# Forgetting attention in a two-layer decoder trunk: query products and the minus of weight pieces at other places in a hand-written order

## Chip, cores and metric

One core of a Trainium2 chip. The metric is the device time of one execution in microseconds (us), as the median of several runs.

## What is computed

The program is a whole two-layer decoder trunk on a residual stream of 512 tokens and 1024 features: a layer with dilated window attention and a gated convolutional feed-forward part, then a layer with forgetting attention and a second feed-forward part. The change lies in the forgetting attention. Cut to that part (16 heads of 64, blocks of 128 queries):

```python
def fox_mixer(xn, w_q, w_o, k, v, c):
    q = (xn @ w_q).reshape(B, T, B_HEADS, HEAD_DIM)
    ...
    for i in range(T // BLK):
        q0, q1 = i * BLK, (i + 1) * BLK
        s = jnp.einsum('bqhd,bkhd->bhqk', q[:, q0:q1], k[:, :q1]).astype(jnp.float32) * scale
        s = s + (c_t[:, :, q0:q1, None] - c_t[:, :, None, :q1])
        s = jnp.where(causal, s, NEG)
        p = jax.nn.softmax(s, axis=-1).astype(v.dtype)
        outs.append(jnp.einsum('bhqk,bkhd->bqhd', p, v[:, :q1]))
    o = jnp.concatenate(outs, axis=1)
    return o.reshape(B, T, B_WIDTH) @ w_o
```

Keys, values and the cumulative log-forget gates `c` are computed once, ahead of it.

## The kernel before

**Numbers.** Every float32 factor of a large product is split into a high part and a low part (the rest), and a product is three matmuls: high with high, high with low, low with high (`mm3`, lines 264 to 266). So each operand costs a copy on ACT (the high part) and a subtraction on DVE (the low part).

**Weights.** The class `Weights` hands out the weights in pieces of 128 x 1024. `load` issues the DMA of a raw piece on SP's queue; `high` copies it on ACT (line 57); `low` subtracts on DVE (line 69). In place of `low` there is a second way: `minus` writes the raw piece times -1 into the place of the low part on ACT (line 64), rounded as the high part is, and `low_added` issues a DMA on POOL's queue that adds the raw piece onto it (line 84), which leaves raw minus high. The four calls stand by hand in the attention loop.

**The loop.** A unit is (j, i): pair of heads j (0 to 7) and query block i (0 to 3), 32 units, in this order, and one pass of the loop issues for each unit, engine by engine in the order of the code (the schedule is manual, so each engine works in exactly this order):

- at i = 0, on SP: the load of the next pair's gates (`load_ck`);
- at i = 2, on PE: a part of the query product, then the 24 score matmuls (line 1578): 12 for blocks 2 and 3 of pair j, and 12 for blocks 0 and 1 of pair j + 1, and then the value products of the units finished so far (`values_of`, line 1627, 40 matmuls);
- on DVE: the reciprocal and the norm of the unit before (`f_norm`, lines 1598 and 1600);
- `f_exp`: on DVE the bias is added and the minimum taken (line 1588), on ACT the exponential with its sum (line 1590), for the two heads;
- on POOL: the bias of the next unit (`f_bias`, lines 1560 and 1561);
- the weight calls and the drains of the query product: `q_high` (ACT, line 1500) and `q_low` (DVE, line 1506);
- at i = 0, 1 and 3, on PE: one part of a query product;
- `f_transpose` of the unit two back: transposes on PE (line 1612) and the copies of the transposed probabilities on ACT (line 1614);
- copies of finished outputs, `f_out_high` on ACT (line 1637) and `f_out_low` on DVE (line 1641).

A query product for one pair is 24 matmuls in four parts of six (`q_part`, lines 264 to 266 with the tile `q_ps`):

```python
        for kc in (2 * i, 2 * i + 1):
            bh, bl = xs(xTq, kc, ALL)
            mm3(o, wh[:, kc, :], wl[:, kc, :], bh, bl, kc == 0, kc == KD - 1)
```

The parts serve as filling between the pieces of the attention, ahead of their pair: in the kernel before, three parts of pair 1 run ahead of the loop, and from there on the last part of pair j + 1 runs in (j,0), and three parts of pair j + 2 in (j,1), (j,2) and (j,3). After the last part `q_high` stands at the end of (j,0) and `q_low` in (j,1). From (6,1) on no part is left; from (6,3) on parts of the output projection (`po.both`, tile `acc`) fill the units.

**What is shared.** All tiles in PSUM, the query products, scores, transposes and outputs, take one of eight banks; the attention's tiles in SBUF (gates, bias, probabilities, raw pieces) take one of ten slots. A tile's first writer waits until the last reader of the slot's or bank's earlier tile is done.

Of the kernel before, what the change touches and what calls it, by code (L numbers as in the profile page):

```python
# [103 lines left out]
def trunk_kernel(ctx, tc, x, norm_gains, w_qkv_a, w_o_a, w_q_b, w_o_b, kv_norm, w_kvf, b_f,  # L104
# [11 lines left out]
    def t8(shape, dt=F32, name="t8"):  # L116
        return p8.tile(shape, dt, tag="t8", name=name)
# [4 lines left out]
    def t2(shape, dt=F32, name="t2"):  # L122
        return p2.tile(shape, dt, tag="t2", name=name)

    def bank(shape, name="bank"):
        return psp.tile(shape, F32, tag="ps", name=name)
# [76 lines left out]
    W = Weights(nc, new_raw, lambda: t8([128, 2, 1024], F32R, name="w"), pieces)  # L203
# [59 lines left out]
    def mm3(o, ah, al, bh, bl, first, last, shared=False):  # L263
        pe.matmul(o, ah, bh, start=first, stop=False, skip_group_check=shared)  # L264
        pe.matmul(o, ah, bl, start=False, stop=False, skip_group_check=shared)  # L265
        pe.matmul(o, al, bh, start=False, stop=last, skip_group_check=shared)  # L266
# [91 lines left out]
    def xs(xT, kc, s):  # L358
        return xT[0][kc // 4][:, kc % 4, s], xT[1][kc // 4][:, kc % 4, s]
# [1116 lines left out]
    def load_ck(j):  # L1476
        t = t4([128, 2, T], name="ck")
        s = cd[2 * j:2 * j + 2, :]
        sp.dma_start(t, bass.AP(tensor=s.tensor, offset=s.offset, ap=[[0, 128], [T, 2], [1, T]]))
        cks[j] = t  # L1480
# [4 lines left out]
    def q_part(j, i):  # L1485

        if j >= 8:
            return
        if i == 0:
            qps[j] = (bank([128, T], name="q_ps"), [t.rearrange("p (k c) -> p k c", k=8) for t in W.get()])  # L1490
        o, (wh, wl) = qps[j]
# [4 lines that stand above are left out]
    def q_high(j):  # L1496
        if j >= 8:
            return
        qT[j] = t8([128, 2, T], F32R, name="qst")
        act.copy(qT[j][:, 0], qps[j][0])  # L1500

    def q_low(j):
        if j >= 8:
            return
        o, t = qps.pop(j)[0], qT[j]
        dve.tensor_tensor(t[:, 1], o, t[:, 0].bitcast(F32), ALU.subtract)
# [48 lines left out]
    def f_bias(j, i):  # L1555
        n = (i + 1) * 128
        bias = t4([128, 2, T], name="bias")
        for hh in range(2):
            hd = 2 * j + hh
            pool.tensor_scalar(bias[:, hh, :n], cks[j][:, hh, :n], -1.0, cq[:, i, hd:hd + 1], ALU.mult, ALU.add)  # L1560
        pool.affine_select(bias[:, :, n - 128:n], bias[:, :, n - 128:n], pattern=[[0, 2], [-1, 128]],
                           compare_op=ALU.is_ge, fill=NEG, base=0, channel_multiplier=1)
        bia[j, i] = bias
# [3 lines left out]
    def f_scores(j, blocks):  # L1567
        wide = blocks[0] >= 2
        if not wide:
            both = [bank([128, 2, 256], name="s_ps") for _ in range(2)]  # L1570
        k = kst[j // 2][:, j % 2]
        for i in blocks:
            nn = max(256, (i + 1) * 128)
            sc[j, i] = [bank([128, T], name="s_ps") for _ in range(2)] if wide else [o[:, i] for o in both]
            for qp, kp in ((0, 0), (0, 1), (1, 0)):
                for hh in range(2):
                    own = slice(64 * hh, 64 * hh + 64)
                    pe.matmul(sc[j, i][hh][:, :nn], qT[j][own, qp, i * 128:(i + 1) * 128], k[own, kp, :nn],
                              start=qp + kp == 0, stop=qp == 1)

    def f_exp(j, i):
        n = (i + 1) * 128
        s = sc.pop((j, i))
        bias = bia.pop((j, i))
        p = t4([128, 2, T], name="prob")
        nm, ls = small(2, "nm"), small(2, "ls")
        for hh in range(2):
            dve.tensor_tensor_reduce(p[:, hh, :n], s[hh][:, :n], bias[:, hh, :n], -0.125, BIG, ALU.add, ALU.min,
                                     nm[:, hh:hh + 1])
            act.activation(p[:, hh, :n], p[:, hh, :n], AF.Exp, bias=nm[:, hh:hh + 1], scale=-1.0,  # L1590
                           accum_out=ls[:, hh:hh + 1])
        prob[j, i] = (p, ls)

    def f_norm(j, i):
        n = (i + 1) * 128
        p, ls = prob[j, i]
        rl = small(2, "rl")
        dve.reciprocal(rl, ls)
        for hh in range(2):
            dve.tensor_scalar(p[:, hh, :n], p[:, hh, :n], rl[:, hh:hh + 1], None, ALU.mult)  # L1600
# [3 lines left out]
    def f_transpose(j, i):  # L1604
        p, _ = prob.pop((j, i))
        for hh in range(2):
            if i >= 2 or hh == 0:
                o = bank([128, 4, 128], name="pT_ps")
                t = t2([128, 4, 128], name="pT")
            k0 = (i + 1) * hh if i < 2 else 0  # L1610
            for k in range(i + 1):
                pe.transpose(o[:, k0 + k, :], p[:, hh, k * 128:(k + 1) * 128], ident)  # L1612
            if i >= 2 or hh == 1:
                act.copy(t[:, :k0 + i + 1], o[:, :k0 + i + 1])
            pT[j, i, hh] = t[:, k0:k0 + i + 1]
# [16 lines left out]
    def f_out_high(j):  # L1632
        o = ops[j]
        if j % 2 == 0:
            OTb[j // 2] = t8([128, 2, 2, T], F32R, name=f"OTb{j // 2}")
        t = OTb[j // 2]
        act.copy(t[:, 0, j % 2, :], o)

    def f_out_low(j):
        o, t = ops.pop(j), OTb[j // 2]  # L1640
        dve.tensor_tensor(t[:, 1, j % 2, :], o, t[:, 0, j % 2, :].bitcast(F32), ALU.subtract)
# [3 lines left out]
    wo = W.n_get + 7  # L1645
    fill = [(kc, b) for b in range(2) for kc in range(4)]
    W.ahead, W.ahead_dma = 1, 1
    for i in range(3):
        q_part(1, i)
        if i == 0:  # L1650
            W.split(W.n_get + 1)
# [6 lines left out]
    def values_of(n):  # L1658
        nonlocal pv_next
        while pv_next < n - 2:  # L1660
            j, i = units[pv_next]
            pv_next += 1
            f_pv(j, i)
            if i == 3:
                outs.append(j)

    f_scores(0, (0, 1))
    for n in range(N + 3):
        live = n < N
        if live:  # L1670
            j, i = units[n]
            if i == 0 and j + 1 < 8:
                load_ck(j + 1)
            if i == 2:
                q_part(j + 2, 1)
                f_scores(j, (2, 3))
                if j + 1 < 8:
                    f_scores(j + 1, (0, 1))
                values_of(n)
        if 1 <= n <= N:  # L1680
            f_norm(*units[n - 1])
        if live:
            f_exp(j, i)
            if n + 1 < N:
                f_bias(*units[n + 1])
            if i == 1:
                q_low(j + 1)
                if 2 <= j < 6:
                    W.minus()
                    W.low_added()  # L1690
            if i == 2 and j < 2 or (j, i) >= (6, 2):
                W.low()
            if i == 3 and j:
                f_out_low(j - 1)
            if i != 2:
                q_part(j + 1 + (i > 0), (i + 3) % 4)
            if (j, i) in ((7, 1), (7, 2)):
                next(down1)
        if 2 <= n < N + 2:
            f_transpose(*units[n - 2])  # L1700
        if n >= N + 3 - len(fill):
            po.both(*fill[n - N - 3 + len(fill)])

        if n >= N and n % 4 in (0, 2):
            values_of(n)
        while outs:
            f_out_high(outs.pop())
        if live and i == 0:
            q_high(j + 1)
        if live and (i == (j < 2) if j < 6 else (j, i) >= (6, 1) and W.n_split < wo + 4):  # L1710
            W.high()

    for _ in range(2):
# [51 lines left out]
```

## Time and profile before

| | |
|---|---|
| median of 3 runs | 1112.32 us (1112.14 to 1112.51) |
| the profiled execution: its time | 1111.92 us |
| the profiled execution: its span | 1110.1 us, 18038 instructions |
| mean granted clock of TensorE | 0.998 |
| PE, DVE, ACT, POOL busy | 1100.2, 876.4, 660.5, 213.8 us |
| query products of the attention (tile `q_ps`) | first matmul at 597.3 us, last at 698.2 us of the span |

The profile is of one execution; its times are counted from the first instruction of the span. A row of a timeline gives the start, the duration, the engine, the line, the operation, the output and inputs by their names, the shape and how many instructions were merged; in brackets stands how long the engine was idle before and what ended that. PE is TensorE's matmuls, whose ends are modelled; ACT is ScalarE, DVE is VectorE, POOL is GpSimd, SP the engine that issues most DMAs. A row of the windows view gives a stretch, then for PE, weight loads, DVE, ACT and POOL the busy time and the number of instructions, then the granted clock, the busy share of the DMA engines and GB/s.

### The profile page before, as it was taken

What the parts mean: (1) busy time and instruction counts of PE and PEld (TensorE: products, weight loads), DVE (VectorE), ACT (ScalarE), POOL (GpSimd) and SP (SyncE); (2) the same over time, 40 slices, a digit from 0 to 9 for tenths busy, and PEclk for the clock granted to TensorE, in tenths of its full rate; (3) what the DMA queues carried; (4) which work ended last, traced back from release to release, by engine and by line L of the source; (5) the groups of instructions that cost most, each with busy time, mean ns of one, the idle gap of its engine ahead of it and who ended that gap; (6) DMA issues with size and microseconds to landing.
All of it is one profiled execution on the core that took longest, in us unless ns stands there. A gap on an engine that the chain in (4) does not pass through costs nothing. (4 is left out here: it accounts for less than half of the span.)

```text
span 1110.1 us, 18038 instructions
## 1 busy us (share of the span) xinstructions
PE 1100.2 (99%) x6610; PEld 954.0 (86%) x6610; DVE 876.4 (79%) x1484; ACT 660.5 (59%) x1088; POOL 213.8 (19%) x313
## 2 busy tenths in 40 slices
PE   9999999999999999999999999999999999999997
PEld 6988889899999988888878888789999999988886
DVE  6687788888788689997686676868887788779994
ACT  5444565656666747576451587746556666747572
POOL 2833000311111211000000445500411111211000
PEclk9999999999999999999999999999999999999999
DMA  9599854378978979794448444584368878989862
GB/s 326 172 341 409 323 183 135 84 180 193 211 186 188 241 264 327 286 324 112 133 152 285 157 110 122 176 276 117 83 179 211 192 183 195 228 268 318 318 247 76
DMA packets 184242, 236.26 MB, mean 213 GB/s; under 512 B 11673, under 2 KB 131465, under 8 KB 184154
## 3 DMA queue, kind: packets, MB, share of 16 engines
q1 hardware_dynamic: 169210, 182.94, 50.2%
q0 software_dynamic: 14944, 52.18, 20.5%
q8 instruction: 52, 0.85, 0.3%
q14 instruction: 36, 0.29, 0.1%
HBM read 166.08 MB, written 39.63 MB: 185 GB/s over the span
## 5 line engine op out<-in xcount | busy, mean ns | idle before, releaser
L264 PE MATMUL acc<-w 128*128 128x512 f32 (+1 forms) x311 | 120.6, 388 | 0.3 <-DVE mix L326 0.3
L266 PE MATMUL acc<-w 128*128 128x512 f32 (+1 forms) x311 | 120.4, 387 | 0.0
L69 DVE TENSOR_TENSOR w<-wraw,w 128x1024 fp32r<-128x1024 f32 x74 | 97.4, 1334 | 24.6 <-ACT w L57 24.0
L57 ACT CAST w<-wraw 128x1024 fp32r<-128x1024 f32 x94 | 96.9, 1049 | 20.9 <-PE v_ps L265 6.9
L265 PE MATMUL acc<-w 128*128 128x512 f32 (+1 forms) x267 | 103.2, 387 | 0.0
L264 PE MATMUL up<-xsh,w 128*128 128x256 f32 x352 | 99.6, 283 | 0.0
L265 PE MATMUL up<-xsl,w 128*128 128x256 f32 x352 | 99.6, 283 | 0.0
L266 PE MATMUL up<-xsh,w 128*128 128x256 f32 x352 | 99.6, 283 | 0.0
L614 ACT ACTIVATE bb<-up,conv 128x512 f32<-128x512 f32 x80 | 59.6, 775 | 58.4 <-DVE up L1001 47.6
L265 PE MATMUL up<-xcl,w 128*128 128x512 f32 (+1 forms) x276 | 93.5, 339 | 0.0
L265 PE MATMUL up<-xbl,w 128*128 128x512 f32 (+1 forms) x276 | 93.5, 339 | 0.0
L264 PE MATMUL up<-xbh,w 128*128 128x512 f32 (+1 forms) x276 | 93.5, 339 | 0.0
L264 PE MATMUL up<-xch,w 128*128 128x512 f32 (+1 forms) x276 | 93.5, 339 | 0.0
L266 PE MATMUL up<-xbh,w 128*128 128x512 f32 (+1 forms) x276 | 93.4, 338 | 0.0
L266 PE MATMUL up<-xch,w 128*128 128x512 f32 (+1 forms) x276 | 93.4, 338 | 0.0
L264 PEld LDWEIGHTS acc<-w 128*128 128x128 f32 x311 | 58.4, 188 | 12.6 <-DVE mix L326 0.7
L266 PEld LDWEIGHTS acc<-w 128*128 128x128 f32 x311 | 58.4, 188 | 11.9
L264 PEld LDWEIGHTS up<-xsh,w 128*128 128x128 f32 x352 | 67.6, 192 | 0.0
L265 PEld LDWEIGHTS up<-xsl,w 128*128 128x128 f32 x352 | 67.6, 192 | 0.0
L266 PEld LDWEIGHTS up<-xsh,w 128*128 128x128 f32 x352 | 67.6, 192 | 0.0
L615 DVE SCALAR_TENSOR_TENSOR bb<-up,conv,bb 128x511 f32<-128x511 f32 x80 | 59.5, 744 | 5.7 <-ACT bb L614 5.6
L617 DVE SCALAR_TENSOR_TENSOR bb<-up,conv,bb 128x510 f32<-128x510 f32 x80 | 59.9, 749 | 2.8
(313 smaller groups left out, 3120.2 us busy)
## 6 DMA issues: line engine op xcount, KB each, us to landing
wraw<-in_w_up_dram SPq DMA_DIRECT2D x88, 512.0 KB, 5.2
w<-wraw POOLq DMA_DIRECT2D x32, 512.0 KB, 6.4
dT<-dsums SPq DMA_DIRECT2D x28, 512.0 KB, 7.7
w<-wsum POOLq DMA_DIRECT2D x24, 512.0 KB, 5.8
dsums<-in_w_down_dram SPq DMA_DIRECT2D x22, 512.0 KB, 7.5
dsums<-in_w_down_dram SPq DMA_DIRECT2D x44, 256.0 KB, 5.5
hD<-hc POOLq DMA_DIRECT2D x44, 256.0 KB, 6.6
dact<-hD SPq DMA_DIRECT2D x44, 256.0 KB, 5.9
```

What stands on the lines that cost most here:

```text
L57: self.nc.scalar.copy(pair[:, 0], raw)
L69: self.nc.vector.tensor_tensor(pair[:, 1], raw, pair[:, 0].bitcast(F32), ALU.subtract)
L264: pe.matmul(o, ah, bh, start=first, stop=False, skip_group_check=shared)
L265: pe.matmul(o, ah, bl, start=False, stop=False, skip_group_check=shared)
L266: pe.matmul(o, al, bh, start=False, stop=last, skip_group_check=shared)
L614: act.activation(bb[:, s, :], ps, AF.Identity, bias=cp[:, 3, ch:ch + 1], scale=cp[:, 2, ch:ch + 1])
L615: dve.scalar_tensor_tensor(bb[:, s, 1:], ps[:, :T - 1], cp[:, 1, ch:ch + 1], bb[:, s, 1:], ALU.mult, ALU.add)
L617: dve.scalar_tensor_tensor(bb[:, s, 2:], ps[:, :T - 2], cp[:, 0, ch:ch + 1], bb[:, s, 2:], ALU.mult, ALU.add)
```

## The change

All parts of the query products run one unit later: two parts of pair 1 stay ahead of the loop in place of three, and in the loop parts 2 and 3 of pair j + 1 run in (j,0) and (j,1), parts 0 and 1 of pair j + 2 in (j,2) and (j,3). `q_high` and `q_low` both stand in (j,1) behind the last part, after the exponentials of that unit and ahead of the copies of transposed probabilities. The weight calls move a unit later as well (copy in (j,1), for pairs 0 and 1 in (j,2)); for pairs 2 to 5 `minus` and `low_added` move from (j,1), where they stood ahead of the copies of probabilities, to (j,2), behind them. Nothing is added or left out.

```diff
-    for i in range(3):
+    for i in range(2):
         q_part(1, i)
...
             if i == 2:
-                q_part(j + 2, 1)
+                q_part(j + 2, 0)
                 f_scores(j, (2, 3))
...
             f_exp(j, i)
             if n + 1 < N:
                 f_bias(*units[n + 1])
-            if i == 1:
-                q_low(j + 1)
-                if 2 <= j < 6:
-                    W.minus()
-                    W.low_added()
-            if i == 2 and j < 2 or (j, i) >= (6, 2):
+            if i == 3 and j < 2 or (j, i) >= (6, 2):
                 W.low()
             if i == 3 and j:
                 f_out_low(j - 1)
             if i != 2:
-                q_part(j + 1 + (i > 0), (i + 3) % 4)
+                q_part(j + 1 + (i > 1), (i + 2) % 4)
+            if i == 1:
+                q_high(j + 1)
+                q_low(j + 1)
...
         if 2 <= n < N + 2:
             f_transpose(*units[n - 2])
+        if live and i == 2 and 2 <= j < 6:
+            W.minus()
+            W.low_added()
...
         while outs:
             f_out_high(outs.pop())
-        if live and i == 0:
-            q_high(j + 1)
-        if live and (i == (j < 2) if j < 6 else (j, i) >= (6, 1) and W.n_split < wo + 4):
+        if live and (i == 1 + (j < 2) if j < 6 else (j, i) >= (6, 1) and W.n_split < wo + 4):
             W.high()
```

## The prediction

> **What bounds the kernel now.** The page comes first. Its row of engines, then two rows of the windows view from the end of the attention loop:
>
> ```profile
> PE 1100.2 (99%) x6610; PEld 954.0 (86%) x6610; DVE 876.4 (79%) x1484; ACT 660.5 (59%) x1088; POOL 213.8 (19%) x313
> ...
> 700.00:710.00 10.00, 9.29 (x88) 7.31 (x87) 9.07 (x26) 9.47 (x26) 6.02 (x11) 1.00 0.65 207
> 710.00:720.00 10.00, 9.51 (x81) 6.98 (x80) 8.10 (x28) 7.20 (x20) 3.79 (x5) 1.00 0.45 167
> ```
>
> PE is busy for all but 9.9 us of the span. The change adds and removes no matmul, so it moves the time only by the holes it closes or opens on PE. In the windows that hold pair 6 and the first half of pair 7, PE is busy 9.29 and 9.51 of 10 us, the clock column stays at 1.00, and DVE and ACT come to 9.07 and 9.47 of 10: there the softmax chain (DVE minimum, ACT exponential, DVE norm) sets the pace. I write (j,i) for pair j, block i, and T(j,i) for the transposes of its probabilities. The PE timeline shows the block of 24 score matmuls in (1,2), (2,2) and (3,2), and the value products that follow it:
>
> ```profile
> 638.50 1.77 PE L1578 MATMUL s_ps<-kst,qst 64*128 64x384 f32 x15
> ...
> 640.78 2.40 PE L1627 MATMUL o_ps<-pT,Vt 128*64 128x128 f32 x40
> ...
> 651.02 1.61 PE L1578 MATMUL s_ps<-kst,qst 64*128 64x384 f32 x13
> 652.86 0.97 PE L1578 MATMUL s_ps<-kst,qst 64*128 64x256 f32 x11 [0.22 <-ACT pT L1614]
> ...
> 664.01 2.73 PE L1578 MATMUL s_ps<-kst,qst 64*128 64x384 f32 x24
> 666.66 2.40 PE L1627 MATMUL o_ps<-pT,Vt 128*64 128x128 f32 x40
> ```
>
> In (1,2) the block takes 640.78 - 638.50 = 2.28 us. In (3,2) it takes 2.65, 0.37 more. In (2,2) the row names the cause: after 13 matmuls, with the second bank of the next pair's scores, PE waits for an ACT copy of probabilities that must free a bank. That copy stands behind the minus of a weight piece in ACT's order:
>
> ```profile
> 651.28 1.06 ACT L64 ACTIVATE w<-wraw 128x1024 fp32r<-128x1024 f32 x1
> 652.23 1.06 ACT L1614 COPY pT<-pT_ps 128x512 f32<-128x512 f32 x2
> ...
> 656.57 0.37 ACT L1614 COPY pT<-pT_ps 128x256 f32<-128x256 f32 x1 [2.08 <-PE pT_ps L1612]
> ...
> 657.31 0.73 ACT L1590 ACTIVATE prob<-prob,nm 128x512 f32<-128x512 f32 x1
> ```
>
> Four turns (j = 2 to 5) have such a hole, so moving the minus is worth 4 x 0.37 = 1.5 us at most. The last two rows show how a turn is tied together: ACT idles 2.08 us until PE reaches T(2,0), and from there copy, exp(2,3) and all that follows run as one chain to the next block of scores.
>
> **Part 1: the minus moves, and the query drain moves with it.** Here is the same turn, T(2,0) to the scores at 664.01, from ACT and then DVE, with an unhindered pair for two gaps (query copy to query low; DVE minimum to exponential):
>
> ```profile
> 661.76 0.59 ACT L1500 CAST qst<-q_ps 128x512 fp32r<-128x512 f32 x1
> 662.24 1.06 ACT L57 CAST w<-wraw 128x1024 fp32r<-128x1024 f32 x1
> 663.19 0.51 ACT L1590 ACTIVATE prob<-prob,nm 128x256 f32<-128x256 f32 x1
> ...
> 664.18 1.06 ACT L64 ACTIVATE w<-wraw 128x1024 fp32r<-128x1024 f32 x1
> ...
> 661.82 0.41 DVE L1588 CUSTOM_DVE_ANT_0 prob<-s_ps,bias 128x256 f32<-128x256 f32 x1
> ...
> 662.50 0.68 DVE L1506 TENSOR_TENSOR qst<-q_ps,qst 128x512 fp32r<-128x512 f32 x1
> ```
> ```profile
> 613.82 0.59 ACT L1500 CAST qst<-q_ps 128x512 fp32r<-128x512 f32 x1 [7.33 <-PE q_ps L266]
> ...
> 614.44 0.69 DVE L1506 TENSOR_TENSOR qst<-q_ps,qst 128x512 fp32r<-128x512 f32 x1 [3.91 <-ACT qst L1500]
> ...
> 626.69 0.41 DVE L1588 CUSTOM_DVE_ANT_0 prob<-s_ps,bias 128x256 f32<-128x256 f32 x1
> ...
> 627.21 0.51 ACT L1590 ACTIVATE prob<-prob,nm 128x256 f32<-128x256 f32 x1 [0.77 <-DVE nm L1588]
> ```
>
> Before, the query low ends at 662.50 + 0.68 = 663.18, well ahead of the scores at 664.01. After, the minus stands between the copy of T(2,0) and the output copy, so exp(2,3) and the chain behind it move by 652.23 - 651.28 = 0.95. The minimum of (3,1) goes from 661.82 to 662.77, and its exponential starts about 0.5 later, at 663.25, since query copy and weight copy no longer stand before it. The unit's two exponentials take 664.18 - 663.19 = 0.99, so the query copy starts at 664.24, the query low 0.62 later (614.44 - 613.82), at 664.86, and ends at 665.54. PE is due at the first score of pair 4 after 12 of 24 matmuls. The row of the eleven small ones lasts 0.97, so twelve take about 1.0 and the twelve larger the rest of 2.28, 1.3: PE is due at 664.01 + 1.3 = 665.3. It needs that query, and banks: eight in all, of which the query product's and the two copies' come free last (the wait at 652.86 was for the first copy's). If the first small score gets the query product's bank, PE waits 0.3 in place of 0.37, and the turn gains 0.1 (0.37 if an earlier bank is dealt to it, -0.2 if the second copy's). I take 0.1, since banks are dealt in the order in which they come free.
>
> Behind the query low on DVE stands the reciprocal of (j,1), and with it norm (j,1), the minimum of (j,2) and its exponential; the weight copy (1.06) moves into the same stretch of ACT. All of it ends in the 2.08 of ACT's idle time ahead of T(j,0), of which about 1 us is left; without that cover exp(j,3) would be late by the excess. SP's load of the next raw piece goes a unit later with the weight copy; it has a whole pair of time before its use, so it costs nothing.
>
> POOL's queue is reordered too. The adding DMA goes behind bias (j,3), which loses its wait, but ahead of bias (j+1,0), which then waits for the later minus:
>
> ```profile
> 652.64 0.90 POOL L84 DMA_DIRECT2D w<-wraw  x1 [3.38 <-PE s_ps L1578]
> ...
> 659.07 0.89 DVE L1600 TENSOR_SCALAR prob<-prob,rl 128x512 f32<-128x512 f32 x2
> ...
> 659.87 0.29 DVE L1588 CUSTOM_DVE_ANT_0 prob<-s_ps,bias 128x128 f32<-128x128 f32 x1
> ...
> 660.48 1.15 POOL L1560 TENSOR_SCALAR bias<-ck,cq 128x384 f32<-128x384 f32 x2 [2.10 <-DVE nm L1588]
> ...
> 697.96 1.32 DVE L1600 TENSOR_SCALAR prob<-prob,rl 128x512 f32<-128x512 f32 x2
> ```
>
> The two instructions of norm (2,3) took 0.89, while POOL was idle (2.10 up to 660.48); those of (5,3) took 1.32, beside bias work. In the changed order the bias of (j+1,0) and (j+1,1) slide to where norm (j,3) stands, which is on the chain. That costs 0 to 0.43 in each of the three turns that start from j = 2, 3, 4; I take 0.2, the middle. So three turns cost 3 x (0.2 - 0.1) = +0.3. The Trainium skill ("SBUF — State Buffer", section "Who interferes with whom") says that a tensor_scalar on DVE and a GpSimd instruction share a port pair that is locked for a whole instruction, the later one blocking fully. By that rule each of the two norm instructions could wait out a bias instruction, at the top of this range or over it; the 0.43 of the trace is about one such wait.
>
> **Part 2: one part less ahead of the loop.** A part is six matmuls. On PE:
>
> ```profile
> 619.06 0.39 PE L264 MATMUL q_ps<-xqh,w 128*128 128x512 f32 x1
> ...
> 620.42 0.39 PE L264 MATMUL q_ps<-xqh,w 128*128 128x512 f32 x1
> ```
>
> 1.36 us later the second part starts, so scores, minimum and exponential of (0,0) come 1.36 earlier. This is a loan: the part returns in (6,1). PE is due at the first scores of pair 2 at 638.50 - 1.36 + 1.3 = 638.4. What must be done by then is the query low of pair 2:
>
> ```profile
> 628.33 0.17 DVE L1598 RECIPROCAL rl<-ls 128x2 f32<-128x2 f32 x1 [0.27 <-ACT prob L1590]
> ...
> 630.36 1.22 DVE L69 TENSOR_TENSOR w<-wraw,w 128x1024 fp32r<-128x1024 f32 x1
> ...
> 638.46 0.69 DVE L1506 TENSOR_TENSOR qst<-q_ps,qst 128x512 fp32r<-128x512 f32 x1
> ```
>
> It ended at 639.15. In its own unit it now follows exponentials and query copy, not the minimum: 0.5 + 1.0 + 0.62 after the minimum's start in place of 0.68 (662.50 - 661.82), so 1.4 later. Against that stands what is left of the 1.36: the reciprocal of (0,1) waits for query low behind query copy (0.62 + 0.6 = 1.2 later than its 628.33 less 1.36), and the weight low (1.22) still lies on DVE before (1,0), only a unit later, where it again delays a reciprocal. So 0.2 to 1.36 is left; I take 0.7. Then the query low ends at 639.15 + 1.4 - 0.7 = 639.85, PE waits 1.4 there, and the loan is spent at once: net 0 (-0.7 to +0.4). In the turn from j = 1 the weight copy and low (0.95 on ACT, 1.22 on DVE) lie in the chain, 0.3 more than a minus: about +0.1.
>
> **Part 3: pair 6, where the loan is paid back.** PE, then DVE:
>
> ```profile
> 694.92 0.44 PE L1612 MATMUL pT_ps<-ident,prob 128*128 128x128 f32 x2
> ...
> 700.06 0.44 PE L1578 MATMUL s_ps<-kst,qst 64*128 64x384 f32 x1
> 700.86 2.64 PE L1578 MATMUL s_ps<-kst,qst 64*128 64x384 f32 x23 [0.36 <-ACT pT L1614]
> 703.44 2.40 PE L1627 MATMUL o_ps<-pT,Vt 128*64 128x128 f32 x40
> ```
> ```profile
> 701.12 0.41 DVE L1588 CUSTOM_DVE_ANT_0 prob<-s_ps,bias 128x256 f32<-128x256 f32 x1
> ...
> 701.81 0.68 DVE L1506 TENSOR_TENSOR qst<-q_ps,qst 128x512 fp32r<-128x512 f32 x1
> ```
>
> Before, no weight work stands between T(5,0) at 694.92 and the scores of pair 7: the piece of pair 5 was done ahead of T(5,0). After, its minus is behind it: the minimum of (6,1) goes to 701.12 + 0.95 = 702.07, and the query low to 702.07 + 0.5 + 1.0 + 0.62 = 704.19, ending at 704.87, against 701.81 + 0.68 = 702.49. PE gets the returned part to do (1.4), so it is due at those scores at about 700.06 + 1.4 + 1.3 = 702.8. It waits until 704.9, then come the 12 scores (1.0), and the value products start at 705.9 in place of 703.44: +2.4. If a bank is free sooner, four scores that need no query low run ahead of it (0.3), and it is +2.1. I take +2.2. Behind it the chain is as before (T(6,0), copy, output copy, weight copy, exponentials), tied to PE again, so nothing is given back; what PE does after 730 us is dense and hides nothing.
>
> **Sum.** 0 (front) + 0.1 (j = 1) + 0.3 (three turns) + 2.2 (pair 6) = +2.6 us. Against the profiled run's own 1111.92 that is 1114.5; the median of the three runs, 1112.32, lies 0.4 above that run, so I say 1114.9.
>
> **Rivals.** *The minus pays and the query drain is in time.* If the chain is 0.3 a turn shorter than I work out, the query low ends before PE is due, the four holes close (-1.5) and the part in (6,1) fills PE's holes there (up to -1.4): -2.9, 1109.4. For it: the drain misses PE by only 0.3 a turn. Against it: pair 6, which misses by 2. Chance 0.05.
>
> *The bank order is kinder.* With early banks each turn gains 0.37 (-1.1 in three), the front keeps 0.7 of its loan, pair 6 costs 2.1, POOL costs nothing: 2.1 + 0.1 - 1.1 - 0.7 = +0.4, 1112.7; half way to it, +1.5. Chance of this region (up to +2.0): 0.28.
>
> *A slot of the landing DMA stalls the chain.* The adding DMA's raw piece becomes a slot for a later probability tile, and it is now issued later, behind T(j,0):
>
> ```profile
> w<-wraw POOLq DMA_DIRECT2D x4, 512.0 KB, 5.1
> ```
>
> The minus behind the copy at 656.57 ends at 656.57 + 0.37 + 1.06 = 658.0, in place of 652.3; 5.1 more is 663.1. The minimum of (3,1) wants its tile at 662.8, that of (3,0) at 660.8 (659.87 + 0.95). If such a tile gets that slot, a turn loses 0.3 to 2.3, four times: 1.2 to 9 on top. Slots, too, are dealt in the order of their release, and the later release makes a later tile likelier. Chance 0.10, typical 1118.
>
> *POOL collides fully*: 0.43 in place of 0.2, three times, and a front that loses 0.4: +3.7, 1116.0. Chance 0.17.
>
> The forecast itself, +2.0 to +3.2, has 0.40.
>
> **How the numbers follow.** A measurement of this kernel tells about 0.2% (2.2 us) from no change. Low: half-kind banks, 1113.3. High: full collision and a little of the slot, 1116.6. Outside lie the first rival, part of the slot's and the far end of the kinder one: 0.2. Faster by over 0.2%: 0.04. Slower: the slot 0.10, collision 0.17, and of the forecast its part over +2.2, 0.32: 0.59. The rest, 0.37, is the kinder banks (0.28), the forecast's lower edge (0.08) and the tame end of the first rival (0.01).
>
> **What would show it.** Right: PE's score blocks in (2,2) to (5,2) still wait, now before their 13th matmul and on the query (ACT L1500, DVE L1506) and not on the copy of probabilities; a wait of over 1 us in (1,2) and near 2 us in (6,2); POOL beside norm (j,3). Wrong: blocks of 2.28 in all turns, or PE waiting on a probability tile's minimum behind a landing DMA.

## The result, and the profile after

| | before | changed |
|---|---|---|
| median | 1112.51 us (7 runs, 1112.07 to 1114.76) | 1116.42 us (7 runs, 1115.37 to 1117.19) |
| ratio | | 1.0035, 95% interval 1.0025 to 1.0045 |
| the profiled execution: time, span | 1111.92, 1110.1 us | 1115.8, 1114.0 us |

The changed kernel is slower by 3.9 us (1116.42 - 1112.51), 1.5 us above the forecast of 1114.9 and inside its range. The page's row of engines and the two windows of the end of the loop, to be held against those of before (PE 9.29 and 9.51 of 10 us, DVE 9.07 and 8.10):

```profile
PE 1101.3 (99%) x6610; PEld 953.7 (86%) x6610; DVE 876.1 (79%) x1484; ACT 661.0 (59%) x1088; POOL 216.7 (19%) x313
...
700.00:710.00 10.00, 9.17 (x88) 7.28 (x87) 7.18 (x25) 7.51 (x21) 7.52 (x14) 1.00 0.64 159
710.00:720.00 10.00, 9.10 (x56) 6.62 (x58) 8.71 (x27) 8.24 (x21) 6.93 (x11) 1.00 0.75 265
```

The same work, the same clock, more holes on PE. The PE timeline of the changed kernel has them in the middle of the score blocks. Here are the blocks in (1,2), (2,2), (3,2) and (6,2) with the value products behind:

```profile
637.58 1.65 PE L1578 MATMUL s_ps<-kst,qst 64*128 64x384 f32 x12
640.00 1.21 PE L1578 MATMUL s_ps<-kst,qst 64*128 64x256 f32 x12 [0.78 <-ACT pT L1614]
641.15 2.40 PE L1627 MATMUL o_ps<-pT,Vt 128*64 128x128 f32 x40
...
651.36 1.50 PE L1578 MATMUL s_ps<-kst,qst 64*128 64x384 f32 x12
653.59 1.21 PE L1578 MATMUL s_ps<-kst,qst 64*128 64x256 f32 x12 [0.73 <-ACT pT L1614]
654.73 2.40 PE L1627 MATMUL o_ps<-pT,Vt 128*64 128x128 f32 x40
...
664.96 1.49 PE L1578 MATMUL s_ps<-kst,qst 64*128 64x384 f32 x12
667.01 1.22 PE L1578 MATMUL s_ps<-kst,qst 64*128 64x256 f32 x12 [0.56 <-ACT pT L1614]
668.16 2.40 PE L1627 MATMUL o_ps<-pT,Vt 128*64 128x128 f32 x40
...
703.42 2.08 PE L1578 MATMUL s_ps<-kst,qst 64*128 64x384 f32 x12
706.14 1.47 PE L1578 MATMUL s_ps<-kst,qst 64*128 64x256 f32 x12 [0.65 <-ACT qst L1500]
707.54 2.40 PE L1627 MATMUL o_ps<-pT,Vt 128*64 128x128 f32 x40
```

In the kernel before, the value products behind the block in (2,2) started here:

```profile
653.76 2.40 PE L1627 MATMUL o_ps<-pT,Vt 128*64 128x128 f32 x40
```

The block in (2,2) takes 654.73 - 651.36 = 3.37 us (before 653.76 - 651.02 = 2.74), the one in (3,2) 3.20 (before 2.65). The one in (1,2) takes 3.57 and the one in (6,2) 4.12, where (1,2) before took 2.28. PE stops after 12 matmuls, not 13, that is ahead of the first score that needs the new query. In (6,2) the row names the query copy (L1500); in the others it names the copy of probabilities (L1614). ACT shows why; beside it DVE and POOL in the turn from T(2,0):

```profile
665.41 0.49 ACT L1590 ACTIVATE prob<-prob,nm 128x256 f32<-128x256 f32 x1
665.91 0.56 ACT L1500 CAST qst<-q_ps 128x512 fp32r<-128x512 f32 x1
666.38 1.07 ACT L1614 COPY pT<-pT_ps 128x512 f32<-128x512 f32 x2
...
661.05 1.25 DVE L1600 TENSOR_SCALAR prob<-prob,rl 128x512 f32<-128x512 f32 x2
...
663.71 0.82 DVE L1600 TENSOR_SCALAR prob<-prob,rl 128x128 f32<-128x128 f32 x2
664.46 0.41 DVE L1588 CUSTOM_DVE_ANT_0 prob<-s_ps,bias 128x256 f32<-128x256 f32 x1
...
666.50 0.69 DVE L1506 TENSOR_TENSOR qst<-q_ps,qst 128x512 fp32r<-128x512 f32 x1 [1.29 <-ACT qst L1500]
...
659.23 0.90 POOL L84 DMA_DIRECT2D w<-wraw  x1 [7.15 <-ACT w L64]
659.88 1.03 POOL L1560 TENSOR_SCALAR bias<-ck,cq 128x128 f32<-128x128 f32 x2
...
661.38 1.26 POOL L1560 TENSOR_SCALAR bias<-ck,cq 128x256 f32<-128x256 f32 x2
...
663.11 1.16 POOL L1560 TENSOR_SCALAR bias<-ck,cq 128x384 f32<-128x384 f32 x2
```

The query copy now stands between the exponentials and the copies of probabilities, so the first copy, which frees the bank, ends only at about 666.9, and the query low at 667.19. And two norms, of (2,3) and of (3,0), stand beside bias work of POOL: 1.25 and 0.82 us, where before they took 0.89 and 0.53.

To compare kernels I take the starts of T(j,0) on PE. What lies ahead of the attention is the same in all of them, yet the first query product starts between 597.0 and 598.8 us in the profiled executions; the first column is counted from there (before 597.30, changed 597.63). "End" is the first matmul behind the loop.

| us | to T(1,0) | T(1,0) to T(2,0) | to T(3,0) | to T(4,0) | to T(5,0) | to T(6,0) | to the end |
|---|---|---|---|---|---|---|---|
| before | 45.81 | 12.98 | 12.91 | 12.96 | 12.96 | 10.85 | 24.24 |
| changed | 45.85 | 13.59 | 13.42 | 13.22 | 13.21 | 12.95 | 24.03 |
| e1 query only | 45.77 | 13.19 | 14.25 | 14.25 | 14.22 | 12.88 | 24.33 |
| e2 minus behind | 45.82 | 12.37 | 13.21 | 12.95 | 14.18 | 10.98 | 24.38 |
| e3 added late | 45.83 | 13.63 | 12.87 | 12.75 | 12.76 | 12.52 | 24.01 |
| e4 drain early | 44.99 | 12.91 | 12.70 | 12.50 | 12.49 | 11.82 | 23.78 |
| e5 both | 44.94 | 12.86 | 12.37 | 12.33 | 12.38 | 11.38 | 23.90 |
| e6 early, old weights | 44.91 | 12.40 | 12.36 | 12.39 | 14.29 | 12.13 | 24.37 |
| e7 pair 5 late | 45.83 | 13.61 | 12.86 | 12.75 | 12.75 | 12.75 | 24.11 |
| e8 three ahead | 47.68 | 13.61 | 13.38 | 13.21 | 13.18 | 12.93 | 24.01 |
| e9 pair 5 clean | 45.83 | 14.09 | 12.88 | 12.75 | 12.75 | 12.56 | 24.34 |
| e10 e5, pair 5 clean | 44.96 | 13.34 | 12.37 | 12.34 | 12.37 | 11.40 | 24.25 |
| e11 e6, no adding | 44.92 | 12.36 | 12.40 | 12.35 | 12.40 | 10.96 | 24.23 |
| e12 low later | 45.83 | 13.05 | 13.20 | 13.20 | 13.18 | 12.94 | 24.01 |

Changed against before: +0.04, +0.61, +0.51, +0.26, +0.25, +2.10, -0.21, together +3.56; with the 0.33 that this execution lost ahead of the attention it is the whole difference between the two profiled times, 1115.80 - 1111.92 = 3.88.

### The profile page after: what moved, and what is told of

It is laid out like the page before. It is cut to its first block, busy times and chain, and to the rows that moved or that the text cites. A ratio compares the mean times of both kernels' runs of the same rounds, so it can differ in the third digit from the quotient of the medians.

```text
span 1114.0 us, 18053 instructions
## 1 busy us (share of the span) xinstructions
PE 1101.3 (99%) x6610; PEld 953.7 (86%) x6610; DVE 876.1 (79%) x1484; ACT 661.0 (59%) x1088; POOL 216.7 (19%) x313
```

## The experiments

Theory: the query drain behind the exponentials is late for the scores, and POOL's bias work stretches norms on the chain. Rivals: the minus in the chain after T(j,0) is the loss; or the landing of the adding DMA. (The drain of a query product is its query copy and query low.) Every kernel was timed against the kernel before, whose median was 1112.31 in the first four, 1112.27 in e5 to e8, 1112.09 in e9 to e11 and 1112.39 in e12. Differences against the changed kernel are between medians of different sessions (1112.51 was the kernel before in its own), so 0.1 to 0.4 of them can be the session's. The table above is of one execution each.

**e1: the query moves, the weight calls stay at the places of before** (against the changed kernel).

```diff
+            if i == 1 and 2 <= j < 6:
+                W.minus()
+                W.low_added()
...
             if i == 1:
                 q_high(j + 1)
                 q_low(j + 1)
...
-        if live and i == 2 and 2 <= j < 6:
-            W.minus()
-            W.low_added()
```

W.low and W.high went back to their old units too.

> The query products run as in the changed kernel, the weight calls stand where they stood before (copy in (j,0), minus ahead of the copies of probabilities in (j,1)). Drain theory (the query copy and low behind the exponentials of (j,1) make PE wait): most of the loss stays, +2.5 to +3.5 us over the kernel before, about 1115.5; the waits ahead of the small scores of (2,2) to (5,2) stay 0.5 to 1 us, pair 6 costs about 1.4 in place of 2.1. Minus theory (the minus behind T(j,0) lengthens the chain): it is gone here, so 0 to +0.5. POOL theory (the bias work beside norm (j,3)): the norm of (j,3) is back near 0.9 us and the loss falls to about +2.

Measured: 1118.39, ratio 1.0055 (1.0042 to 1.0067): 6.1 us over the kernel before, worse than the whole change and beyond what either theory expected. With the minus left where it was, both it and the query copy lie ahead of the copies, and PE waits twice as long:

```profile
664.10 1.50 PE L1578 MATMUL s_ps<-kst,qst 64*128 64x384 f32 x12
666.98 1.22 PE L1578 MATMUL s_ps<-kst,qst 64*128 64x256 f32 x12 [1.38 <-ACT pT L1614]
```

Norm (2,3) is back at 1.01 here, against 1.25, and yet the time rose, so the theory of POOL alone falls for this kernel. The move of the weight calls, the minus among them, is not the loss; it gives back about 2 us of what the query's move costs.

**e2: the minus moves alone** (against the kernel before).

```diff
             if i == 1:
                 q_low(j + 1)
-                if 2 <= j < 6:
-                    W.minus()
-                    W.low_added()
+            if i == 2 and 2 <= j < 6:
+                W.low_added()
...
             f_transpose(*units[n - 2])
+        if live and i == 1 and 2 <= j < 6:
+            W.minus()
```

> The kernel before, with nothing changed but the minus: it stands in (j,1) behind the copies of probabilities, and the adding DMA behind the bias of (j,3). Drain theory and the reading of the holes: the four waits of about 0.4 us ahead of the second small score vanish and nothing takes their place, -1.5 us, about 1111.0. Rival (the bank is not what holds PE, or the minus costs the same wherever it stands): 0 +- 0.4.

Measured: 1113.15, 1.0010 (1.0002 to 1.0019), where 1.5 less was expected. The holes in the score blocks are gone (653.12 - 650.98 = 2.14 in (2,2), and the first turn takes 12.37), but a new wait takes their place, at the third matmul of the product that uses the piece:

```profile
650.98 2.21 PE L1578 MATMUL s_ps<-kst,qst 64*128 64x384 f32 x24
653.12 2.40 PE L1627 MATMUL o_ps<-pT,Vt 128*64 128x128 f32 x40
...
659.84 0.40 PE L265 MATMUL q_ps<-xql,w 128*128 128x512 f32 x1
660.83 0.50 PE L266 MATMUL q_ps<-xqh,w 128*128 128x512 f32 x1 [0.60 <-DMA w<-wraw]
...
687.95 0.50 PE L266 MATMUL q_ps<-xqh,w 128*128 128x512 f32 x1 [1.53 <-DMA w<-wraw]
```

The adding DMA, one bias later on POOL, lands too late: in three turns this matmul starts 0.5 to 1.7 us later than the 0.23 behind its neighbour that is usual. My gain of 1.5 forgot that landing. POOL's bias waited for it too, 5.1 to 6.7 us, and DVE's minima for that bias, up to 2.0; e6 shows more of this.

**e3: the adding DMA behind the bias of (j+1,0)** (against the changed kernel).

```diff
+            if i == 3 and 2 <= j < 6:
+                W.low_added()
...
             W.minus()
-            W.low_added()
```

> The changed kernel, with the adding DMA of POOL behind the bias of (j+1,0), which then waits for no minus; the minus stays on ACT where it is. POOL theory: norm (j,3) falls from about 1.25 to 0.9 - 1.0 us and each of the turns by 0.3, so -1.0 to -1.4 us against the changed kernel, about +2.7 over the one before (1115.2). Drain theory alone (the norm is covered): no change, +3.9.

Measured: 1113.73, 1.0012 (1.0004 to 1.0021), 2.7 under the changed kernel, more than expected. Between the two profiled executions the attention is 1.9 shorter, 1.47 of it in the three turns and 0.43 in pair 6; the rest of the 2.7 lies in how far each of these two executions was from its median. The bias of (j+1,0) no longer waits for the minus, the later ones mostly move off the norms:

```profile
660.95 1.03 DVE L1600 TENSOR_SCALAR prob<-prob,rl 128x512 f32<-128x512 f32 x2
663.39 0.48 DVE L1600 TENSOR_SCALAR prob<-prob,rl 128x128 f32<-128x128 f32 x2
```

1.25 and 0.82 have become 1.03 and 0.48, together 0.56 less, and the turn is 0.55 shorter. The norms account for the whole gain of that turn.

**e4: last part and query copy ahead of the exponentials of (j,1), query low behind the minima** (against the changed kernel).

```diff
+            if i == 1:
+                q_part(j + 1, 3)
+                q_high(j + 1)
             f_exp(j, i)
...
-            if i != 2:
+            if i in (0, 3):
                 q_part(j + 1 + (i > 1), (i + 2) % 4)
             if i == 1:
-                q_high(j + 1)
                 q_low(j + 1)
```

> The changed kernel, with the last part of a query product and the query copy issued ahead of the exponentials of (j,1), and the query low right behind the two minima. Drain theory: query low done 1 us earlier, ahead of the small scores; the waits of (1,2) to (5,2) fall to 0.3 or less and pair 6 gains 1 us or more, so that the total is within 1 us of the kernel before (1111.5 to 1113.5). POOL and minus theories: the chain that starts at T(j,0) keeps its length, at least +2 stays (1114.5 or more).

Measured: 1111.21, 0.9989 (0.9980 to 0.9998), 5.2 under the changed kernel and 0.3 under what the drain theory expected. From (3,2) on the blocks run through, although the minus and POOL's collisions are still there:

```profile
664.57 2.51 PE L1578 MATMUL s_ps<-kst,qst 64*128 64x384 f32 x24
667.01 2.40 PE L1627 MATMUL o_ps<-pT,Vt 128*64 128x128 f32 x40
```

**e5: e3 and e4 together.**

> The changed kernel with both mends together: last query part and query copy ahead of the exponentials of (j,1) and the query low right behind its minima, and the adding DMA behind the bias of (j+1,0). Apart they measured -5.2 us (drain early) and -2.5 us (adding DMA late) against the changed kernel. If the two losses sit in the same chain and the early drain already leaves slack in turns j = 3 to 5, the norm's stretching is paid out of that slack, and the two together are worth little over the early drain alone: -1.1 to -2.0 us against the kernel before, 1110.3 to 1111.2. If they are separate losses that add, three turns gain 0.4 each again and the time is 1109.4 to 1110.0. A third way: with less on the chain PE comes sooner to the third matmul of the query part, and waits there for the adding DMA, now issued 1.2 us later; then 0.5 to 2 us worse than the early drain alone, 1111.7 to 1113.2.

Measured: 1109.61, 0.9975 (0.9964 to 0.9986): 2.7 under the kernel before, a small gain but clear of its interval. Turns of 12.37, blocks of 2.13:

```profile
663.06 2.20 PE L1578 MATMUL s_ps<-kst,qst 64*128 64x384 f32 x24
665.19 2.40 PE L1627 MATMUL o_ps<-pT,Vt 128*64 128x128 f32 x40
```

The time lies in the range that was expected for losses that add, yet they do not add up in full: the two mends alone came to 7.9, together they bring 6.8 (7.0 and 6.1 in the sums of the table). That both shorten one chain would explain it, and was not tested by itself.

**e6: the early drain with the weight calls a unit sooner** (copy in (j,0), minus in (j,1) behind the copies, adding DMA behind the bias of (j,3), and the subtractions of pairs 0 and 1 a unit sooner).

```diff
+            if i == 2 and 2 <= j < 6:
+                W.low_added()
...
-        if live and i == 2 and 2 <= j < 6:
+        if live and i == 1 and 2 <= j < 6:
             W.minus()
-            W.low_added()
...
-        if live and (i == 1 + (j < 2) if j < 6 else ...
+        if live and (i == (j < 2) if j < 6 else ...
```

> The early drain with the weight calls one unit sooner than in the changed kernel: copies of pieces in (j,0), minus in (j,1) behind the copies of probabilities, the adding DMA behind the bias of (j,3). The piece has one unit more between its adding DMA and its first use than in the kernel before with the minus moved alone, so PE should not wait for its landing; pair 6 has no minus in its chain (about -0.95 there), and POOL no bias beside norm (j,3). The theory (three separate losses: drain, minus in the chain of pair 6, POOL beside the norm) expects -1.5 to -2.5 us against the kernel before, 1109.8 to 1110.8, with no wait on a weight piece at the query products and a norm (j,3) of 0.89 us. The rival (PE is only as early as the softmax chain lets it, and the early drain has already taken all slack there was) expects the same as the early drain alone, -1.1, 1111.2.

Measured: 1113.71, 1.0009 (1.0000 to 1.0017), with runs from 1111.97 to 1115.57, where 1109.8 to 1110.8 was expected. The profiled execution is the fastest of them. Three of its turns are at 12.4, the fourth is 14.29. The waits view of the loop:

```profile
POOL bias L1560 <- DMA w<-wraw: 22.0, 4, 7.2
...
DVE prob L1588 <- POOL bias L1561: 5.8, 4, 3.2
```

The bias of (j+1,1) waits for the adding DMA, whose data it does not use: by the rule of the slots it has been dealt the slot of the raw piece that the DMA still reads. The DVE minimum waits for that bias, once 3.2 us. This is the prediction's slot rival, in another kernel. The transfers took 7.3 us here:

```profile
w<-wraw POOLq DMA_DIRECT2D x4, 512.0 KB, 7.3
```

in the changed kernel 4.6, in e2 7.5.

**e11: e6 without the four adding DMAs of the loop** (the low parts of four pieces stay at minus the raw piece).

```diff
-            self.nc.gpsimd.dma_start(pair[:, 1], raw, accum_op=ALU.add)
+            if add:
+                self.nc.gpsimd.dma_start(pair[:, 1], raw, accum_op=ALU.add)
```

> The early drain with the weight calls one unit sooner, with the four adding DMAs in the loop left out (the low parts of four weight pieces stay at minus the raw piece). In the run with them (1113.71) the bias of (j+1,1) on POOL waited 4 to 7 us for their landing, since it takes the slot of the raw piece, and in pair 5 the minimum waited 3.2 us for that bias. If this landing is the whole loss and also the cause of that kernel's spread (1111.97 to 1115.57), all turns come to 12.4 us, the time to 1109 to 1110, and the spread falls under 1.5 us. If the loss is in the order of the weight calls itself (copy and minus in ACT's chain), the time stays over 1111.5.

Measured: 1109.65, 0.9975 (0.9966 to 0.9985), runs from 1108.55 to 1110.77. All four turns are 12.4 and pair 6 is 10.96. So the adding DMAs are the whole loss of e6. This run takes out their issue on POOL along with their landing; that it is the landing is read from the waits above. The spread fell from 3.6 to 2.2, not under 1.5, so a part of it has another cause.

**e7 and e9: does the minus count in pair 6?** e7 is e3 with pair 5's minus and adding DMA a unit later, at (5,3); e9 has that adding DMA behind the bias of (6,1) as well.

```diff
-        if live and i == 2 and 2 <= j < 6:
+        if live and (i == 2 and 2 <= j < 5 or (j, i) == (5, 3)):
             W.minus()
```

> The changed kernel with the adding DMA late (which measured 1.4 us over the kernel before), and in pair 5 alone the minus and its adding DMA one unit later, behind the copies of (5,3)'s pass, so that no minus stands between T(5,0) and the scores of pair 7. Part 3 of the prediction put 0.95 us of pair 6's loss on that minus (and 1.2 to 1.4 on the query drain and the returned part). By it: 0.95 less, +0.4 to +0.6 us over the kernel before, 1112.7 to 1112.9, and the minimum of (6,1) about 0.95 earlier against T(5,0). By the rival (the query drain alone sets pair 6's wait, or the minus of the later unit delays the same chain elsewhere): no change, +1.2 to +1.6, 1113.5 to 1113.9.

> The kernel with pair 5's minus one unit later (the run before of that name measured 1114.01, and the minimum of (6,1) waited 0.83 us there for a bias that stood behind the adding DMA on POOL), now with pair 5's adding DMA behind the bias of (6,1) too, so that this bias waits for nothing. If the minus in the chain of pair 6 is worth what the prediction's part 3 gave it, the minimum of (6,1) stands 0.8 to 1.0 us closer to T(5,0) than the 6.71 us it had with the adding DMA late alone, and the time falls by as much: 1112.7 to 1113.1. If the chain of pair 6 is bounded elsewhere (the query copy behind the exponentials alone), it stays at 1113.6 to 1114.0.

Measured: 1114.01, 1.0015 (1.0006 to 1.0024), and 1114.37, 1.0017 (1.0009 to 1.0026): no gain in either. The minimum of (6,0) comes 1.1 sooner after T(5,0) (e9: 699.61 - 695.83 = 3.78, e3: 700.23 - 695.35 = 4.88): the 0.95 that was worked out, and 0.14 from norm (5,3), which takes 0.89 in place of 1.03. Then POOL takes it back: in e7 the minimum of (6,1) waits 0.83 for a bias behind the adding DMA, and in e9 the norm of (6,0) stands beside the DMA's issue and that bias:

```profile
701.05 1.62 DVE L1600 TENSOR_SCALAR prob<-prob,rl 128x128 f32<-128x128 f32 x2
...
700.31 0.89 POOL L84 DMA_DIRECT2D w<-wraw  x1 [2.52 <-ACT w L64]
700.93 1.46 POOL L1560 TENSOR_SCALAR bias<-ck,cq 128x384 f32<-128x384 f32 x2
```

1.62 in place of 0.48: 1.14 lost for 1.1 won, and pair 6 takes 12.56 against 12.52. The theory's number for the start of the chain held, its number for the time fell; what pair 6 would take without the minus and without the collision was not measured.

**e10: e5 with e9's place for pair 5.**

> The best kernel so far (early drain and late adding DMA, 1109.61) with pair 5's minus and adding DMA placed as in the run above. In that kernel the scores of pair 7 wait only about 0.3 us in all, so whatever the minus is worth in the chain, PE has little left to gain there: 0 to -0.4, 1109.2 to 1109.6, if a PE bound holds in pair 6; -0.9, 1108.7, if the chain alone sets the pace of pair 6; over 1110 if the later adding DMA is late for the output projection that uses the piece.

Measured: 1110.29, 0.9980 (0.9971 to 0.9989); pair 6 takes 11.40 against 11.38: nothing gained, with a norm (6,0) of 1.61, as in e9. The end takes 24.25 against 23.90; there a weight load of the output projection waits 0.3 for the adding DMA, the case that was expected to lead over 1110. Its turn from T(1,0), which has the same code as e5's, took 13.34 in place of 12.86. The norm of (2,0) there, e10 first, then e5, each with the bias beside it:

```profile
649.71 1.10 DVE L1600 TENSOR_SCALAR prob<-prob,rl 128x128 f32<-128x128 f32 x2
...
649.36 1.37 POOL L1560 TENSOR_SCALAR bias<-ck,cq 128x512 f32<-128x512 f32 x2 [1.33 <-PE pT_ps L1612]
```
```profile
649.31 0.62 DVE L1600 TENSOR_SCALAR prob<-prob,rl 128x128 f32<-128x128 f32 x2
...
648.97 1.45 POOL L1560 TENSOR_SCALAR bias<-ck,cq 128x512 f32<-128x512 f32 x2 [1.34 <-PE pT_ps L1612]
```

The bias starts 0.35 ahead of the norm in one and 0.34 in the other; one norm takes 0.48 more than the other, and the turn 0.48 more. The long turn of e9 (14.09) has a norm (2,0) of 1.13 as well.

**e8: three parts ahead of the loop again, none in (0,0).**

```diff
-    for i in range(2):
+    for i in range(3):
...
-            if i != 2:
+            if i != 2 and (j, i) != (0, 0):
```

> The changed kernel with three parts of pair 1 ahead of the loop again and none in (0,0); everything else as changed. The prediction said that the part taken away from the front is a loan which the query drain of the first turn uses up at once, leaving a chain that starts 1.36 us earlier. If that chain sets the pace from the front on, this kernel loses 1.36 us less the 0 to 0.7 that PE waits anyway: +0.7 to +1.4 us against the changed kernel, 1117.0 to 1117.8, with T(1,0) that much later. If the part ahead of the loop costs nothing because the chain waits for something else, the time is that of the changed kernel, 1116.0 to 1116.4.

Measured: 1117.70, 1.0048 (1.0035 to 1.0062), 1.3 over the changed kernel between the medians; in the profiled execution T(1,0) is 1.83 later and the turns behind it are unchanged. The chain sets the pace from the front on.

**e12: pair 1's subtraction from (1,3) to (2,0).**

```diff
-            if i == 3 and j < 2 or (j, i) >= (6, 2):
+            if (j, i) in ((0, 3), (2, 0)) or (j, i) >= (6, 2):
                 W.low()
```

> The changed kernel with the subtraction (DVE, 1.23 us) of pair 1's weight piece one unit later, from (1,3), ahead of the norm of that unit, to (2,0), behind the minima. The turn from T(1,0) to T(2,0) grew from 12.98 to 13.59 us with the change, where the prediction had 0.1 more; in the changed kernel norm (1,3) starts only when this subtraction and an output subtraction are done, and takes 1.38 us beside a bias that waited for the same subtraction. If these make the turn long: norm (1,3) starts about 0.6 us sooner and takes 0.9 to 1.0, 0.4 of that is given back at norm (2,0), and the turn falls to 12.9 to 13.2; the time to 1115.7 to 1116.1. If the turn is long by the weight copy on ACT and the query copy behind the exponentials alone, it stays at 13.5 to 13.6 and the time at 1116.4.

Measured: 1114.92, 1.0027 (1.0015 to 1.0038), 0.8 below the lower end of what I expected. The turn falls from 13.59 to 13.05. First e12, then the changed kernel:

```profile
648.49 0.88 DVE L1600 TENSOR_SCALAR prob<-prob,rl 128x512 f32<-128x512 f32 x2
...
649.71 1.22 DVE L69 TENSOR_TENSOR w<-wraw,w 128x1024 fp32r<-128x1024 f32 x1
...
648.98 2.40 POOL L1560 TENSOR_SCALAR bias<-ck,cq 128x384 f32<-128x384 f32 x2 [2.45 <-DVE prob L1600]
```
```profile
645.80 1.23 DVE L69 TENSOR_TENSOR w<-wraw,w 128x1024 fp32r<-128x1024 f32 x1 [0.81 <-ACT w L57]
...
647.73 1.38 DVE L1600 TENSOR_SCALAR prob<-prob,rl 128x512 f32<-128x512 f32 x2
...
647.13 1.16 POOL L1560 TENSOR_SCALAR bias<-ck,cq 128x384 f32<-128x384 f32 x2 [1.67 <-DVE w L69]
```

Norm (1,3) takes 0.88, against 1.38 in the changed kernel. The turn behind it falls too, from 13.42 to 13.20, where those from j = 3 and 4 stood already: part of the subtraction's cost reached into the turn from j = 2. This time POOL pays: its bias takes 2.40 beside the norm and the subtraction, against 1.16.

## Why the prediction came near, point by point

The sum was +2.6, the attention measured +3.56: +0.04 for 0 at the front, +0.61 for +0.1, +1.02 for +0.3, +2.10 for +2.2, and -0.21 behind pair 6, where the prediction gave nothing back.

**Front: right.** Worked out: query low of pair 2 ended at 639.85, loan spent, net 0. Measured: it ends at 639.50 + 0.69 = 640.19, 0.33 of which is the late start of that execution, and T(1,0) moved by 0.04. e8 shows that without the loan the front would have lost 1.83 in the profiled execution.

**The turn from j = 1: too small, 0.1 against 0.61.** The subtraction of pair 1's piece was counted as part of 0.3 more in the chain. It delays the norm behind it and pushes it beside a bias that had waited for the same subtraction (1.38 against 0.95 before). e12 moves only that and gets 0.54 of the 0.61 back.

**The three turns: too small, +0.3 against +1.02.** The step that failed is "I take 0.2, the middle" for the norm. POOL's slide reached two norms in a turn, not one: in the turn from j = 2 norm (2,3) took 0.36 more than before and norm (3,0) 0.29 more, 0.65 together; in the next two turns it was 0.58 and 0.55. That is 1.78 in place of 0.6. e3 shows the cause: with the bias work out of the way these turns are 1.47 shorter.

The turns grew by less than the norms, so the rest of them became shorter, by 0.14, 0.32 and 0.30, where the prediction took a gain of 0.1 at the banks. This second error hid part of the first, which is luck. One reason is in the blocks. The prediction took 2.28, the block of (1,2), as a block without a hole, and so 0.37 for a hole. Blocks without a wait take 2.13 or 2.14 (e5, e2), so the hole in (2,2) was 2.74 - 2.14 = 0.60, and e2's first turn is shorter by as much, 0.61. "1.5 us at most" for the four holes was therefore too low. The bank was another one, too: PE went on at 667.01, when the first copy was done, and did not wait for the query low (667.19), as it would have for the query product's bank. How much of the gain each of the two brings was not measured.

What the view of before could have told: the bias units that follow the adding DMA in POOL's queue all slide with it, and two of them meet a norm. The Trainium skill ("SBUF — State Buffer", section "Who interferes with whom") says that whichever of the two engines comes later blocks for the other's whole instruction, where the DVE instruction runs in a two-port mode, which a tensor_scalar can enter; no run here shows the mode. The rows 1.62 for 0.48 and, the other way round, 2.40 for 1.16 agree with it better than the middle value did.

**Pair 6: right, +2.2 against +2.10.** The minimum of (6,1) was put at 702.07 - 694.92 = 7.15 after T(5,0), and stands at 704.07 - 696.92 = 7.15; the query low was put at 9.27, and stands at 9.20:

```profile
706.12 0.69 DVE L1506 TENSOR_TENSOR qst<-q_ps,qst 128x512 fp32r<-128x512 f32 x1 [1.29 <-ACT qst L1500]
```

PE began the small scores at 706.14, ahead of the end of this instruction, which is the case that the prediction put at +2.1. The collision with POOL does not show in this difference, since it stood there before as well: norms (5,3) and (6,0) took 1.32 and 0.52, and now 1.22 and 0.74. An earlier drain takes 1.1 of the loss away (e4 against the changed kernel, and e5 against e3). Whether the minus's 0.95 is to be had back is not shown: e7 and e9 take it out of the chain, and POOL takes it back.

**The signs and the rivals.** The blocks wait ahead of their 13th matmul in all turns, those of (1,2) and (6,2) are 1.3 and 1.8 us longer than 2.28, and POOL stands beside norm (j,3), as was said. The wait was put down to the query in (6,2) alone; in the turns it was put down to the copy behind the query in ACT's order, so there the sign was named one instruction too early. The rival that came true is the full collision with POOL (1116.0, chance 0.17). Its cause is the one that e3 shows, but that its time lies so near is partly luck: it had 0.43 a turn and 0.4 at the front, and measured were 0.55 to 0.65 in the norms, nothing at the front, and 0.5 more than forecast in the turn from j = 1. The fast rival (minus pays, drain in time, 1109.4) is near what e5 measured, 1109.61, with a drain some tenths sooner and POOL out of the way, but not by the same parts: there the three turns gain 1.75 and pair 6 still costs 0.53. The slot did not stall the changed kernel; e6 shows its price where it does, 1.9 us in one turn.

Still open: why the profiled executions reach the attention up to 1.7 us apart, and which of two almost equal starts of norm and bias wins.

## What to carry to other kernels

When an instruction is moved past others on an in-order queue, price everything that follows it there, and ask of each what stands beside it at its new time: here the DMA that moved was harmless, and the bias work that slid behind it cost 1.9 us on another engine in the profiled execution, 2.7 between the medians. Moving a drain behind the critical pair of instructions costs the wait of whoever needs the drain and also of everything that queues behind it on the same engine. A transfer put later must be checked at both ends, at its first reader (e2) and at the tile that takes its source's slot (e6).

## What the hardware showed unexpectedly

DVE and POOL, working on SBUF at the same time, stretched each other by far more than a share: a pair of small DVE norms went from 0.48 to 1.62 us beside POOL, and a POOL bias from 1.16 to 2.40 beside DVE. Starts that differ by 0.01 us gave 0.62 or 1.10 for the same norm. And the same 512 KB adding DMA took 4.6 us or 7.3 to 7.5, depending on the order around it. In e2 and e6, the two slow ones, a load of the next raw piece is issued 2.3 to 3.0 us behind each of the first three, in the changed kernel 3.5 and in the kernel before 4.0, which may be the reason and was not tried. The load in e6, behind a DMA issued at 652.64, then in the changed kernel:

```profile
655.07 0.38 SPq L49 DMA_DIRECT2D wraw<-in_w_q_b_dram  x1
```
```profile
662.78 0.38 SPq L49 DMA_DIRECT2D wraw<-in_w_q_b_dram  x1
```
